# Row-wise cosine similarity: a split first load, separate half sums, and another engine that frees y

## The chip, the cores and the metric

The kernel runs on one core of a Trainium2 chip. The core has a TensorE (PE in the profile), a VectorE (DVE), a ScalarE (ACT), a GpSimd (POOL) and a SyncE (SP), which run their own instruction streams and meet through semaphores, and 16 DMA engines that move data between the HBM and the SBUF. The metric is the time of one execution on the device in microseconds (us), here the median of three runs.

## The reference

```python
def reference(x, y):                    # both 8192 x 8192 float32
    x_norm = np.linalg.norm(x, axis=1, keepdims=True)
    y_norm = np.linalg.norm(y, axis=1, keepdims=True)
    return np.sum(x * y, axis=1) / (x_norm.squeeze() * y_norm.squeeze() + 1e-8)
```

For every row three sums are needed: of x squared, of y squared, and of x times y. Each input element is read once; the inputs are 537 MB together, the output is 32 KB.

## The kernel before

**Tiling.** The 8192 rows are cut into 64 blocks of 128. The first 60 blocks are worked on in 30 groups of two blocks: each of the 128 partitions holds two neighbouring rows, 16,384 values or 65,536 bytes, so that one load brings 8.4 MB. The loads alternate, x of a group, then y of it, and go into three SBUF buffers `slot0` to `slot2` in turn (load m goes to slot m % 3). The last four blocks (b = 0 to 3) have one row to a partition; x lies in the first half of a slot and y in the second, and they are loaded in pieces (`PIECES`): whole halves at first, 13 pieces from 3968 down to 384 columns in the last block.

**Who does what.** ScalarE squares and sums x and y (`square`, L142, the ACTIVATE with its accumulator read). VectorE multiplies x with y and sums (`dot`, L145), and writes its products over x. The two rows of a partition have to give two separate sums, and a slot has to come free early: so VectorE first copies the last 4096 values of x into the PSUM tile `side` (L212). When y has come, it works off the middle 4096 values (second row, first half, into `part`), the first 8192 (first row), and then `side` with the last 4096 of y. The last of these starts from `part`, so that its sum is that of the whole second row. After the second of the three dots nothing reads x any more, and `used` tells SP that the slot is free. After the third dot, and when ScalarE has squared y, VectorE increments `used` for y's slot (L223).

**Loops and tokens.** The main part is four hardware loops over R = 10 rounds of three groups (nine rounds on SP), one on each of SP, TensorE, ScalarE and VectorE. `take` (L139) waits for a semaphore and takes the amount off again. SP takes one `used` for each load that it issues. TensorE, which has no arithmetic there, waits for each landing and hands a token to ScalarE (`for_act`) and one to VectorE (`for_dve`). ScalarE takes its token, squares the two halves of the slot, waits for each, and increments `x_squared` or `y_squared`; VectorE waits for `x_squared` ahead of the first dot, because this overwrites x, for its own `partial` around the last dot, and for `y_squared` at the end.

**After the loops.** Waits and increments are counted by hand (class `Queue`): `wait` is queued on an engine in program order, `done` gives an instruction's mark. SP issues the last blocks' loads when slots come free (`take_slot`: blocks 0 to 2 by `used` at 4, 5 and 6, block 3 by the marks of block 0). During block 0 the groups' results are made: the root of the square sums on ScalarE (L340), then on VectorE the product of the norms, plus EPS, the reciprocal (`reciprocal`, L263 to L270) and the multiplication with the dots (L344), two transposes on TensorE (L350), and two copies out of the PSUM on VectorE (L353). After block 2, ScalarE issues their store (L357). In the last block, after piece 4, the denominators of blocks 0 to 2 are made in the same way. The last piece's dot starts from the sum of the pieces before (`base`, L300), and short steps on ScalarE, VectorE and TensorE lead to the last store on SP.

**The opening.** `first_load_and_last_wait` moves the first load's DMA instruction into the opening block of the program, ahead of the barrier of all engines there, and the waits for the stores into the closing block.

The lines that a sentence can't say:

```python
    def take(engine, s, n=1):
        engine.wait_ge(s, n).then_inc(s, -n)
...
                dot(xt[:, K:CUT], yt[:, K:CUT], part, xt[:, K:CUT]).then_inc(partial, 1)
                dot(xt[:, 0:K], yt[:, 0:K], gsum[:, XY, r, c:c + 1], xt[:, 0:K]).then_inc(
                    used, 1)
```

## Time and profile before

| | |
|---|---|
| median of three runs | 1249.38 us (1249.23 to 1249.70) |
| the profiled execution | 1249.41 us, of which its span 1247.6 us |
| ScalarE busy | 916.9 us, 73% of the span |
| VectorE busy | 698.2 us, 56% |
| TensorE, GpSimd busy | 1.3 us, 0.8 us |
| share of 16 DMA engines' span taken by the loads' packets | 99.6% |
| HBM read | 536.87 MB, 430 GB/s over the span |
| a square of 8192 values, a dot of 8192, a dot of 4096, the copy of 4096 | 7.03, 8.69, 4.43, 4.43 us |

The page of a profile gives each engine's busy time, the span in 40 slices, the DMA queues, the chain of work that ended last, and the costliest groups of instructions with the idle time ahead of each and what ended it. A timeline lists instructions in order: start, duration (both in us), engine, line of the kernel, operation, operands, and in brackets the idle time before it with its releaser. SPq and ACTq are instructions of these engines' sequencers: a DMA's issue, a wait, a branch. A DMA's issue has a duration there, but the data move afterwards. A window's row gives, for a stretch of time, busy times of the engines, and at the end the DMA engines' share and the GB/s, where a packet counts whole at its start.

### The profile page before, as it was taken

What the parts mean: (1) busy time and instruction counts of PE and PEld (TensorE: products, weight loads), DVE (VectorE), ACT (ScalarE), POOL (GpSimd) and SP (SyncE); (2) the same over time, 40 slices, a digit from 0 to 9 for tenths busy, and PEclk for the clock granted to TensorE, in tenths of its full rate; (3) what the DMA queues carried; (4) which work ended last, traced back from release to release, by engine and by line L of the source; (5) the groups of instructions that cost most, each with busy time, mean ns of one, the idle gap of its engine ahead of it and who ended that gap; (6) DMA issues with size and microseconds to landing.
All of it is one profiled execution on the core that took longest, in us unless ns stands there. A gap on an engine that the chain in (4) does not pass through costs nothing. (4 is left out here: it accounts for less than half of the span.)

```text
span 1247.6 us, 1785 instructions
## 1 busy us (share of the span) xinstructions
PE 1.3 (0%) x4; PEld 0.3 (0%) x4; DVE 698.2 (56%) x252; ACT 916.9 (73%) x285; POOL 0.8 (0%) x8
## 2 busy tenths in 40 slices
PE   0000000000000000000000000000000000000000
PEld 0000000000000000000000000000000000000000
DVE  1654576545765447654467544675446755457566
ACT  3686776867768668677686776867868668677888
POOL 0000000000000000000000000000000000000000
DMA  9999999999999999999999999999999999999998
GB/s 435 431 414 435 437 437 437 437 435 435 433 412 437 437 437 437 437 437 435 435 424 420 437 437 437 437 437 437 433 433 412 437 437 437 437 437 437 418 425 335
DMA packets 11575, 536.93 MB, mean 430 GB/s; under 512 B 1299, under 2 KB 1845, under 8 KB 2613
## 3 DMA queue, kind: packets, MB, share of 16 engines
q1 hardware_dynamic: 11528, 536.88, 99.6%
q10 hardware_dynamic: 45, 0.03, 0.0%
q14 instruction: 2, 0.02, 0.0%
HBM read 536.87 MB, written 0.03 MB: 430 GB/s over the span
## 5 line engine op out<-in xcount | busy, mean ns | idle before, releaser
L142 ACT ACTIVATE junk<-slot 128x8192 uint8<-128x8192 f32 (+4 forms) x138 | 900.8, 6528 | 326.2 <-ACTq L139 320.5
L145 DVE CUSTOM_DVE_ANT_0 slot<-slot,slot 128x4096 f32<-128x4096 f32 (+1 forms) x60 | 391.1, 6556 | 452.4 <-DVEq L139 452.4
L212 DVE COPY side<-slot 128x4096 f32<-128x4096 f32 x30 | 132.8, 4428 | 71.7 <-DVEq L139 71.7
L145 DVE CUSTOM_DVE_ANT_0 side<-side,slot,part 128x4096 f32<-128x4096 f32 x30 | 134.6, 4488 | 0.0
L145 DVE CUSTOM_DVE_ANT_0 slot<-slot 128x8192 f32<-128x8192 f32 (+3 forms) x5 | 29.6, 5944 | 20.4 <-ACT junk L142 12.7
L142 ACT ACTIVATION_READ_ACCUMULATOR junk<-slot (+1 forms) x138 | 25.7, 186 | 0.0
L145 DVE CUSTOM_DVE_ANT_0 vjunk<-slot 128x384 uint8<-128x384 f32 (+4 forms) x8 | 6.8, 886 | 1.0 <-DMA slot<-in_y_dram 1.0
L145 DVE DVE_READ_ACCUMULATOR2_ANT gsum<- x60 | 6.7, 112 | 0.0
L145 DVE DVE_READ_ACCUMULATOR2_ANT part<- 128x1 f32 x30 | 2.5, 83 | 0.0
L192 ACT ACT_TABLE_LOAD x1 | 1.3, 1283 | 1.0 <-SPq L168 1.0
L350 PE MATMUL side<-ident,gden 128*30 128x128 f32 x2 | 0.6, 395 | 1196.9 <-DVE gden L344 1196.9
L194 ACT ACT_TABLE_LOAD x1 | 1.3, 1283 | 0.1
L145 DVE DVE_READ_ACCUMULATOR2_ANT parts<- 128x1 f32 x11 | 0.9, 82 | 0.0
L353 DVE COPY orow<-side 30x128 f32<-30x128 f32 x2 | 0.5, 279 | 0.6 <-PE side L350 0.6
L371 ACT COPY dots<-side 4x128 f32<-4x128 f32 x1 | 0.3, 254 | 0.7 <-PE side L369 0.7
L145 DVE CUSTOM_DVE_ANT_0 vjunk<-slot,base 128x384 uint8<-128x384 f32 x1 | 0.6, 619 | 0.1
L381 DVE TENSOR_TENSOR orl<-side,dots 4x128 f32<-4x128 f32 x1 | 0.3, 279 | 0.5 <-PE side L379 0.5
L270 DVE RECIPROCAL gden<-gden 128x60 f32<-128x60 f32 x1 | 0.5, 529 | 0.0
L350 PEld LDWEIGHTS side<-ident,gden 128*30 128x30 f32 x2 | 0.1, 107 | 1196.8 <-issue 1196.8
L369 PE MATMUL side<-ident,bsum 128*4 128x128 f32 x1 | 0.4, 373 | 46.9 <-DVE bsum L145 46.9
L379 PE MATMUL side<-ident,bden 128*4 128x128 f32 x1 | 0.4, 374 | 0.0
L340 ACT ACTIVATE gnorm<-gsum 128x120 f32<-128x120 f32 x1 | 0.3, 302 | 0.0
(25 smaller groups left out, 4.4 us busy)
## 6 DMA issues: line engine op xcount, KB each, us to landing
slot<-in_x_dram SPq DMA_DIRECT2D x3, 4096.0 KB, 29.9
slot<-in_y_dram SPq DMA_DIRECT2D x2, 4096.0 KB, 32.2
slot<-in_y_dram SPq DMA_DIRECT2D x1, 2368.0 KB, 35.8
slot<-in_x_dram SPq DMA_DIRECT2D x1, 1984.0 KB, 32.3
slot<-in_y_dram SPq DMA_DIRECT2D x1, 1728.0 KB, 39.4
slot<-in_y_dram SPq DMA_DIRECT2D x1, 1600.0 KB, 35.7
slot<-in_x_dram SPq DMA_DIRECT2D x1, 1088.0 KB, 37.9
slot<-in_y_dram SPq DMA_DIRECT2D x1, 640.0 KB, 40.2
```

What stands on the lines that cost most here:

```text
L142: return nc.scalar.activation(out=into, in_=src, func=ACTF.Square, accum_out=acc)
L145: return nc.vector.tensor_tensor_reduce(out=into, in0=a, in1=b, scale=1.0, scalar=init, op0=ALU.mult, op1=ALU.add, accum_out=acc)
L192: nc.scalar.memzero(dummy).then_inc(squared, 1)
L194: nc.scalar.sqrt(out=dummy, in_=dummy).then_inc(squared, 1)
L212: nc.vector.tensor_copy(out=side, in_=xt[:, CUT:])
L270: return dve.done(nc.vector.reciprocal(out=den, in_=den))
L340: m_norm = act.done(nc.scalar.activation(out=gnorm, in_=flat(gsum)[:, 0:2], func=ACTF.Sqrt))
L350: mk = pe.done(nc.tensor.transpose(out=t, in_=gden[:, j:2 * G:2], identity=ident))
L353: rows.append(dve.done(nc.vector.tensor_copy(out=orow[:, :, j], in_=t)))
L369: m_xy = pe.done(nc.tensor.transpose(out=psl[0], in_=bsum[:, XY, :], identity=ident))
L371: m_dots = act.done(nc.scalar.copy(out=dots, in_=psl[0]))
L379: mk = pe.done(nc.tensor.transpose(out=psl[1], in_=bden, identity=ident))
```

## The change

- The first load is cut into 16 partitions (`HEAD`) and 112, two DMAs with a semaphore each, and both issues are moved into the opening block. TensorE waits for the first semaphore once, ahead of its loop.
- The middle dot writes to a column of its own per group (`gpart`) in place of `part`; the last dot of a group starts from zero. GpSimd adds `gpart` to the second rows' sums once, at the end.
- In VectorE's loop the waits for `partial`, `x_squared` and `y_squared` and the increment of `used` for y go. The copy increments `x_done`, the last dot `y_done`.
- ScalarE's loop waits for its first half alone; the second increments `x_done` or `y_done`.
- TensorE takes two of `x_done` before it hands on the tokens for a y, two of `y_done` after that, and then increments `used` for y's slot.
- ScalarE waits for `used` to reach 6 before it goes on to the last blocks.
- The product of the norms and the addition of EPS go from VectorE to GpSimd (`denominator`), as does the multiplication of the groups' results; the reciprocals stay on VectorE, that of the groups in block 1, that of the last blocks after piece 6.
- The two copies of the groups' rows go from VectorE in block 0 to ScalarE after block 2, ahead of the store's issue.

```diff
-    load = next(i for i in body.instructions if i.opcode == "DMACopy")
+    loads = [i for i in body.instructions if i.opcode == "DMACopy"][:2]
...
-    opening.instructions = head[:at] + [load] + head[at:]
+    opening.instructions = head[:at] + loads + head[at:]
...
+    HEAD = 16
...
-        load(xg[0, 0], 0)
+        nc.sync.dma_start(out=slots[0][0:HEAD], in_=xg[0, 0, 0:HEAD]).then_inc(first, 16)
+        nc.sync.dma_start(out=slots[0][HEAD:], in_=xg[0, 0, HEAD:]).then_inc(landed[0], 16)
...
+        nc.tensor.wait_ge(first, 16)
         with nc.tensor.Fori(0, R):
             for m in range(2 * SLOTS):
                 take(nc.tensor, landed[m % SLOTS], 16)
+                if m % 2:
+                    take(nc.tensor, x_done, 2)
                 nc.tensor.sem_inc(for_act, 1)
                 nc.tensor.sem_inc(for_dve, 1)
+                if m % 2:
+                    take(nc.tensor, y_done, 2)
+                    nc.tensor.sem_inc(used, 1)
...
-                for j in range(2):
-                    square(s[:, j * K:(j + 1) * K], gsum[:, q, r, c + j:c + j + 1]).then_inc(
-                        squared, 1)
-                    take(nc.scalar, squared)
-                nc.scalar.sem_inc(y_squared if m % 2 else x_squared, 1)
+                square(s[:, 0:K], gsum[:, q, r, c:c + 1]).then_inc(squared, 1)
+                take(nc.scalar, squared)
+                square(s[:, K:], gsum[:, q, r, c + 1:c + 2]).then_inc(
+                    y_done if m % 2 else x_done, 1)
...
-                nc.vector.tensor_copy(out=side, in_=xt[:, CUT:])
+                nc.vector.tensor_copy(out=side, in_=xt[:, CUT:]).then_inc(x_done, 1)
                 take(nc.vector, for_dve)
-                take(nc.vector, x_squared)
-                dot(xt[:, K:CUT], yt[:, K:CUT], part, xt[:, K:CUT]).then_inc(partial, 1)
+                dot(xt[:, K:CUT], yt[:, K:CUT], gpart[:, r, a:a + 1], xt[:, K:CUT])
                 dot(xt[:, 0:K], yt[:, 0:K], gsum[:, XY, r, c:c + 1], xt[:, 0:K]).then_inc(
                     used, 1)
-                take(nc.vector, partial)
-                dot(side, yt[:, CUT:], gsum[:, XY, r, c + 1:c + 2], side, part).then_inc(
-                    partial, 1)
-                take(nc.vector, partial)
-                take(nc.vector, y_squared)
-                nc.vector.sem_inc(used, 1)
+                dot(side, yt[:, CUT:], gsum[:, XY, r, c + 1:c + 2], side).then_inc(y_done, 1)
...
+        act.wait((used, 2 * SLOTS))
...
-        def reciprocal(norm, den, squared, dotted):
-
-            dve.wait(squared, dotted)
-            m = dve.done(nc.vector.tensor_mul(out=den, in0=norm[:, 0], in1=norm[:, 1]))
-            dve.wait(m)
-            m = dve.done(nc.vector.tensor_scalar_add(out=den, in0=den, scalar1=EPS))
-            dve.wait(m)
+        def denominator(norm, den, *marks):
+
+            pool.wait(*marks)
+            m = pool.done(nc.gpsimd.tensor_mul(out=den, in0=norm[:, 0], in1=norm[:, 1]))
+            pool.wait(m)
+            return pool.done(nc.gpsimd.tensor_scalar_add(out=den, in0=den, scalar1=EPS))
+
+        def reciprocal(den, mark):
+            dve.wait(mark)
             return dve.done(nc.vector.reciprocal(out=den, in_=den))
...
-                    m_den = reciprocal(bnorm[:, :, 0:last], bden[:, 0:last], m_norm, m_sum)
+                    m_den = denominator(bnorm[:, :, 0:last], bden[:, 0:last], m_norm)
+                if b == last and n == 6:
+                    m_den = reciprocal(bden[:, 0:last], m_den)
...
-                m_g = reciprocal(gnorm, gden, m_norm, marks[-1])
-                dve.wait(m_g)
-                m_g = dve.done(nc.vector.tensor_mul(
+                m_g = denominator(gnorm, gden, m_norm)
+                odd = gsum[:, XY].rearrange("p r (a j) -> p r a j", j=2)[:, :, :, 1]
+                pool.wait(marks[-1])
+                m_odd = pool.done(nc.gpsimd.tensor_add(out=odd, in0=odd, in1=gpart))
+            if b == 1:
+                m_g = reciprocal(gden, m_g)
+                pool.wait(m_g, m_odd)
+                m_g = pool.done(nc.gpsimd.tensor_mul(
                     out=gden, in0=flat(gsum)[:, XY], in1=gden))
...
-                    dve.wait(mk)
-                    rows.append(dve.done(nc.vector.tensor_copy(out=orow[:, :, j], in_=t)))
+                    act_late.append((t, mk, orow[:, :, j]))
...
             if b == 2:
+                for t, mk, into in act_late:
+                    act.wait(mk)
+                    rows.append(act.done(nc.scalar.copy(out=into, in_=t)))
```

## The prediction

> **What bounds the kernel now.** I read the page first (engine shares, the forty slices, the queues), then the timeline of the first 75 us, then that of the last 100 us, then the chain that ended last. From the page:

> ```profile
> span 1247.6 us, 1785 instructions
> PE 1.3 (0%) x4; PEld 0.3 (0%) x4; DVE 698.2 (56%) x252; ACT 916.9 (73%) x285; POOL 0.8 (0%) x8
> ...
> q1 hardware_dynamic: 11528, 536.88, 99.6%
> ```

> The sixteen DMA engines are busy for 99.6% of the span; ScalarE has 27% to spare and VectorE 44%. So the inputs' transfer is the bound, and an edit in the loops counts only if it starves or slows that queue. The start of the timeline gives its pace:

> ```profile
> 0.00 0.41 SPq L150 DMA_DIRECT2D slot<-in_x_dram  x1
> ...
> 22.36 7.03 ACT L142 ACTIVATE junk<-slot 128x8192 uint8<-128x8192 f32 x1 [18.25 <-ACTq L139]
> ...
> 41.73 7.03 ACT L142 ACTIVATE junk<-slot 128x8192 uint8<-128x8192 f32 x1 [4.93 <-ACTq L139]
> ...
> 55.31 0.35 SPq L150 DMA_DIRECT2D slot<-in_y_dram  x1
> ...
> 59.99 0.34 SPq L150 DMA_DIRECT2D slot<-in_x_dram  x1
> 61.03 7.03 ACT L142 ACTIVATE junk<-slot 128x8192 uint8<-128x8192 f32 x1 [4.86 <-ACTq L139]
> 61.13 4.43 DVE L212 COPY side<-slot 128x4096 f32<-128x4096 f32 x1 [1.64 <-DVEq L139]
> ```

> Loads are worked on as they land, at 22.36, 41.73 and 61.03: one load of 128 rows x 65,536 B every 19.33 us, 434 GB/s. With eight rows to an engine that is 2.42 us for a row. A y load was issued into the freed x slot at 55.31, 5.7 us before the running load ended, and the next x load at 59.99: the queue always holds more than it is working on. From the last stage:

> ```profile
> 1227.41 0.19 ACT L142 ACTIVATION_READ_ACCUMULATOR junk<-slot 128x1 f32 x1
> 1227.70 3.51 ACT L142 ACTIVATE junk<-slot 128x3968 uint8<-128x3968 f32 x1
> ...
> 1231.53 2.87 ACT L142 ACTIVATE junk<-slot 128x3200 uint8<-128x3200 f32 x1 [0.22 <-DMA slot<-in_y_dram]
> ...
> 1237.89 1.27 ACT L142 ACTIVATE junk<-slot 128x1280 uint8<-128x1280 f32 x1 [0.26 <-DMA slot<-in_y_dram]
> ...
> 1242.49 0.51 ACT L142 ACTIVATE junk<-slot 128x384 uint8<-128x384 f32 x1
> ...
> 1243.33 0.17 DVE L300 TENSOR_REDUCE base<-parts 128x3 f32<-128x21 f32 x1
> ```

> ScalarE follows the landings with gaps of 0.2 to 0.3 us, and the reduction at 1243.33 needs its last pieces. Here a late ScalarE does cost.

> [...]

> **The change, part by part.** The sum is made against the profiled execution: 1249.41 us, of which 1247.6 are span and 1.8 lie around it. The median of the three runs is 1249.38, the same for this purpose.

> *First load.* One issue of 0.41 us becomes two, the second (0.33 us, by the following issues) also ahead of the opening's barrier. SP therefore issues y's first load some 0.3 us later than at 1.07; x's load ahead of it takes about 20 us, so nothing notices. ScalarE's table loads move by the same 0.3 us, and it waits 18.25 us afterwards. Gain: windows of half a microsecond count 1966 GB/s at 1.0 to 1.5 us, by the start of each packet; that is 15 of the 16 first rows. A shorter issue can bring the first rows forward by no more than its own 0.41 us; I take 0.2, between nothing and 0.4.
> Cost: the first 16 rows go to partitions 0 to 15. [...]
> The other 112 rows are seven for each engine[...]. I take 2.4 and keep 0 and 9.7 for the range. An engine's delay stays: each has the same 0.5 GB share / 16 to move afterwards at the same rate, never idle.
> Sum of this part: 7.7 + 2.4 - 0.2 = +9.9.

> *Loops.* VectorE loses two waits for itself and two for ScalarE in each of 30 groups, ScalarE one wait per load and a semaphore instruction; the sums go to two columns. The dots have the same sizes (4.43, 8.69, 4.49 us). All lies under the transfer: VectorE already idles 1.64 us ahead of its copy and ScalarE 4.9 ahead of each load. Gain nothing. The added waits are TensorE's. For x: ScalarE has squared it at 36.80 and VectorE copied it at 26.88, y lands near 41.7, 4.9 us of cover. For y: VectorE's last dot ends near 59.5, the next x lands at 61.0, 1.5 us of cover. Queued behind that wait are the tokens for both engines on the next x; if the cover went, they would start late by the excess, and the next slots come free later. Even then there is a whole load (19.3 us) issued at 55.31. Nothing.

> *Hand-over.* ScalarE now waits for the sixth `used`, after VectorE's last dot (1182.26), in place of starting at 1179.34: some 3.3 us later. Its four squares and the root then run to about 1211.7, and the third block's x lands at 1213.07; 1.4 us remain. VectorE's dot of block 0 ends near 1198.6 in place of 1195.3, so SP issues the last block's loads from 1198.7. Seven issues of 0.47 bring it to 1202, and it was blocked from 1198.17 to 1214.19 [...] anyway. Nothing.

> *Group results.* VectorE's three operations leave it and three (with the joining addition, four) arrive on GpSimd, which is free. Bounds for each: 0.1 us (its memsets) and 1 us. They start near 1197 and, after the reciprocal, near 1214; ScalarE reads the transposes only after 1227.6. Thirteen microseconds of cover.
> The two row copies go to ScalarE just ahead of the last block: 0.25 us each (the L371 copy of the same kind is 0.25), and the store's issue, 0.64 us at 1222.87, must now wait for them. ScalarE's accumulator read ends at 1227.60; two copies to 1228.1, issue to 1228.75, so the 3968 square starts near 1228.8 and not 1227.70: +1.1. The gaps behind it (0.3 at 3200, 0.25 at 1280, 0.15 over the following) take back about 0.7. The second-last 384 square ends near 1243.5 and not 1243.09, the reduction starts near 1243.6 and not 1243.33: +0.3. Bounds: 0 and 0.6.

> *Last denominators.* Two VectorE operations of 0.17 go to GpSimd; the reciprocal comes after the dot of 1280 columns, ahead of a 0.53 us idle stretch. GpSimd at 0.5 each gives 1239.7, in time. At 1 us each VectorE would be some 0.3 late at the end. I take nothing.

> Sum: 1249.4 + 9.9 + 0.3 = 1259.6 us.

> **The rivals.**
> 1. [...] the 16 rows cost 2.42 us as before. For it: the trace shows 27.1 GB/s per engine[...]. Then only the start and ScalarE's tail remain: 1249.4 - 0.2 + 0.3 = 1249.5, with 1248.8 to 1250.1. This is the not-slower side; it decides if the first 16 rows take below some 5 us.
> 2. *The 112 rows are dealt out in turn*, row 16 + 16t + e to engine e. [...] For it: nothing in the profile excludes an order. [...]
> 3. *TensorE's ordered waits starve the queue.* A token more than 1.5 us late would hold both engines in each of 30 groups. If it ate the whole 5.7 us as well, each further 0.1 us costs 3 us. Against it: a relay of a few semaphore instructions; the timelines show gaps of 0.02 to 0.09 us for such steps. One microsecond beyond the cover would be 1279.

> **How the numbers follow.** [...] engines set the pace 0.34, dealt in turn 0.05, TensorE 0.02; the remaining 0.01 is a start that loses most of the 3.0 us by which the first load lands beyond its 19.33. A difference under 0.2% (2.5 us) is about what a measurement of this kernel can't tell from none. Faster 0.02 (the last case and an unknown of rival 1), same 0.33, slower 0.65. The range takes in rival 1 and the contention's own range: 1248.8 to 1267.

> **What would show it.** Right: ScalarE's first square near 32 us or later in place of 22.36, later loads again at 19.3 us apart, the same lateness at the end. Wrong: a first square at 22 to 23 us. The tail: a 3968 square 1.1 us behind its landing, the reduction waiting for ScalarE. TensorE's step: VectorE's copy starting later than 0.2 us behind ScalarE's square of the same x.

## The result, and the profile after

The changed kernel takes 1270.62 us (median of five runs, 1270.42 to 1270.87) against 1249.39 for the kernel before: 1.0169 times its time, 95% interval 1.0155 to 1.0183, 21.2 us more. The profiled execution has a span of 1268.5 us in place of 1247.6.

From the page of the changed kernel: its span, the engines' busy time, the GB/s of the forty slices (31.7 us each), and the loads' queue. The last line is the GB/s of the kernel before, by its own slices (31.2 us).

```profile
span 1268.5 us, 1634 instructions
PE 1.3 (0%) x4; PEld 0.3 (0%) x4; DVE 694.8 (55%) x245; ACT 916.8 (72%) x287; POOL 4.7 (0%) x14
...
GB/s 223 364 432 432 430 430 432 432 430 432 448 432 434 432 430 430 434 430 432 446 434 434 432 430 430 434 430 430 446 434 436 432 430 430 434 430 430 434 427 331
...
q1 hardware_dynamic: 11544, 536.88, 99.6%
...
GB/s 435 431 414 435 437 437 437 437 435 435 433 412 437 437 437 437 437 437 435 435 424 420 437 437 437 437 437 437 433 433 412 437 437 437 437 437 437 418 425 335
```

The share of the queue's packets, 99.6%, is the same as before, and would suggest that nothing has changed: a packet that is held up counts as busy (by the trace's single packets the first sixteen took 7.52 to 9.25 us each, in the kernel before 2.48 to 3.42). The GB/s tell it. The first slice moved 223 and the second 364, every later one about as much as before. The loss lies in the first 45 us. The timeline of the start of the changed kernel:

```profile
0.00 0.41 SPq L172 DMA_DIRECT2D slot<-in_x_dram  x1
...
0.46 0.40 SPq L173 DMA_DIRECT2D slot<-in_x_dram  x1
...
44.14 7.03 ACT L144 ACTIVATE junk<-slot 128x8192 uint8<-128x8192 f32 x1 [39.57 <-ACTq L141]
...
63.67 7.03 ACT L144 ACTIVATE junk<-slot 128x8192 uint8<-128x8192 f32 x1 [5.09 <-ACTq L141]
...
82.83 7.03 ACT L144 ACTIVATE junk<-slot 128x8192 uint8<-128x8192 f32 x1 [4.72 <-ACTq L141]
82.93 4.43 DVE L222 COPY side<-slot 128x4096 f32<-128x4096 f32 x1 [1.56 <-DVEq L141]
```

The first square starts at 44.14, not 22.36: 21.8 us late. The following two come 19.5 and 19.2 us apart, as before, and VectorE idles 1.56 us ahead of its copy (1.64 before). Windows of the same kernel (start and end, length, busy times of the engines; at the end the clock, the DMA engines' share and the GB/s), and last one of the kernel before:

```profile
2.00:10.00 8.00, 0.00 (x0) 0.00 (x0) 0.00 (x0) 2.44 (x4) 0.34 (x3) 1.00 0.44 74
11.00:21.00 10.00, 0.00 (x0) 0.00 (x0) 0.00 (x0) 0.00 (x0) 0.00 (x0) 1.00 0.81 210
21.00:31.00 10.00, 0.00 (x0) 0.00 (x0) 0.00 (x0) 0.00 (x0) 0.00 (x0) 1.00 0.89 223
...
11.00:21.00 10.00, 0.00 (x0) 0.00 (x0) 0.00 (x0) 0.00 (x0) 0.00 (x0) 1.00 0.98 426
```

A packet counts whole where it starts, so a short window's rate is rough. But where the kernel before moved 426 GB/s from 11 to 21 us, this one moves 210, and 223 in the next ten: not only the first 16 rows are slow, the 112 behind them run at half pace.

The tail of the changed kernel, at the place that the prediction spoke of:

```profile
1248.31 0.19 ACT L144 ACTIVATION_READ_ACCUMULATOR junk<-slot 128x1 f32 x1
1248.40 0.41 ACT L372 COPY orow<-side 30x128 f32<-30x128 f32 x2
1248.84 0.64 ACTq L374 DMA_DIRECT2D out_dram<-orow  x1
...
1249.59 3.51 ACT L144 ACTIVATE junk<-slot 128x3968 uint8<-128x3968 f32 x1 [0.78 <-ACT orow L372]
```

The two copies and the store's issue stand between the squares, and the 3968 square starts 1.09 us after the end of the accumulator read.

### The profile page after: what moved, and what is told of

The parts are those of the page before. It is cut to its first block, busy times and chain, and to the rows that moved or that the text cites. A ratio compares the mean times of both kernels' runs of the same rounds, so it can differ in the third digit from the quotient of the medians.

```text
span 1268.5 us, 1634 instructions
## 1 busy us (share of the span) xinstructions
PE 1.3 (0%) x4; PEld 0.3 (0%) x4; DVE 694.8 (55%) x245; ACT 916.8 (72%) x287; POOL 4.7 (0%) x14
## 3 DMA queue, kind: packets, MB, share of 16 engines
q1 hardware_dynamic: 11544, 536.88, 99.6%
## 5 line engine op out<-in xcount | busy, mean ns | idle before, releaser
L147 DVE CUSTOM_DVE_ANT_0 side<-side,slot 128x4096 f32<-128x4096 f32 x30 | 132.9, 4429 | 0.0
L147 DVE CUSTOM_DVE_ANT_0 slot<-slot 128x8192 f32<-128x8192 f32 (+3 forms) x5 | 29.6, 5944 | 22.8 <-ACT junk L144 22.8
## 6 DMA issues: line engine op xcount, KB each, us to landing
slot<-in_y_dram SPq DMA_DIRECT2D x2, 4096.0 KB, 31.9
```

The source lines that it names most:

```text
L147: return nc.vector.tensor_tensor_reduce(out=into, in0=a, in1=b, scale=1.0, scalar=init, op0=ALU.mult, op1=ALU.add, accum_out=acc)
```

## The experiments

Two theories at the start: the split costs it, by the partitions that each part reaches; or the new waits, the hand-over and the tail hold part of it. Within the first, the slow side could be SBUF or the HBM.

In the kernels with a "written out" loop, VectorE's hardware loop is ten rounds one after the other, with the same work; in those with "fixed sums", its loop is kept, its sums go to a fixed tile, and one or two small copies per round move them on.

**The split undone, and the split alone.** The changed kernel with `load(xg[0, 0], 0)` again, and the kernel before with the split; VectorE's loop is written out in both. Of the second edit the two loads are shown; as in the changed kernel, both issues move into the opening and TensorE waits for `first`.

```diff
-        load(xg[0, 0], 0)
+        nc.sync.dma_start(out=slots[0][0:16], in_=xg[0, 0, 0:16]).then_inc(first, 16)
+        nc.sync.dma_start(out=slots[0][16:], in_=xg[0, 0, 16:]).then_inc(landed[0], 16)
```

> The changed kernel with the first load whole again (one DMA, alone in the opening; no `first`); VectorE's loop is written out round by round, which changes none of its work. Theory (the split alone costs the 21 us, by its partitions): 1249.4, within 0.7, first square near 22.4 us. Rival (the new waits of TensorE, the hand-over or the tail hold part of it): 1255 or more, with a first square still near 22 us. ScalarE's later start on the last block should leave its reduction 0.3 us later than its landings of before.

> The kernel before with the split of 16 and 112 partitions alone (VectorE's loop written out). Theory: the whole loss, 1270.6 within 1, first square near 44 us. Rival (the other edits take part in it): 1265 or less.

Measured: with the first load whole 1251.48 us (1.0015, 1.0008 to 1.0022), first square at 22.66; with the split alone 1272.36 us (1.0184, 1.0167 to 1.0201), first square at 44.12. The split holds the loss of some 20 us. But both are some 2 us above what was expected, and whether the other edits had part in those 2 us was open.

**Another split.** The same 1.05 MB first, but as 2048 columns on all partitions; and the load in two halves of 64 partitions, which isn't shown (both again with VectorE's loop written out):

```diff
-        load(xg[0, 0], 0)
+        nc.sync.dma_start(out=slots[0][:, 0:2048], in_=xg[0, 0, :, 0:2048]).then_inc(first, 16)
+        nc.sync.dma_start(out=slots[0][:, 2048:], in_=xg[0, 0, :, 2048:]).then_inc(landed[0], 16)
```

> The kernel before with its first load split as well, but by columns: 2048 of 16384 columns on all 128 partitions first (the same 1.05 MB), then the rest; both issues in the opening, VectorE's loop written out. Theory (partitions): [...] no loss: 1249.4 within 0.6, first square near 22.4. Rival (two DMAs in a row in the opening, or a small first DMA, cost by themselves): 1255 to 1270.

> The kernel before with its first load split into partitions 0 to 63 and 64 to 127 (VectorE's loop written out). Theory [...]: each half takes twice its time, 38.7 us in place of 19.4, so +19.4: 1268.8, first square near 41.7. Rival (the HBM side: sixteen engines reading sixteen neighbouring rows are what is slow): here an engine has four rows of its own, so little or nothing, 1249 to 1254.

Measured: by columns 1252.80 us (1.0025, 1.0015 to 1.0034), first square at 22.18; by halves 1273.68 us (1.0194, 1.0177 to 1.0211), first square at 43.67. The halves came 5 us above the 1268.8 expected, 3 of which the next experiment finds in the written-out loop. Against that loop alone (1252.55), two DMAs of all partitions cost nothing, two DMAs of 64 partitions 21 us. The first issue takes 0.41 us with 2048 columns as well.

**What the 2 us were.** The kernel before with nothing but the loop written out, and, with the loops kept and fixed sums, the kernel before, the changed kernel with a whole first load, and the same with the split by columns:

```diff
-        with nc.vector.Fori(0, R) as r:
+        for r in range(R):
```

```diff
-                dot(side, yt[:, CUT:], gsum[:, XY, r, c + 1:c + 2], side, part).then_inc(
+                dot(side, yt[:, CUT:], gacc[:, c + 1:c + 2], side, part).then_inc(
...
+            nc.vector.tensor_copy(out=gsum[:, XY, r, :], in_=gacc).then_inc(partial, 1)
+            take(nc.vector, partial)
```

> The kernel before with VectorE's loop written out and nothing else. Theory (the 2 us of the whole-first-load run come from the longer instruction stream, whose fetches take DMA time, and not from the changed waits): 1251.0 to 1251.9, with four or five instruction packets in place of two. Rival (they come from the other edits of the change): 1249.4 to 1249.8.

> The kernel before with its loops kept, VectorE's sums of a round in a fixed tile that one copy per round moves on. The copy lies in VectorE's idle time. Theory (fetches): two instruction packets again, 1249.4 within 0.5. Rival (anything that delays the loops' hand-overs shows at once): 1251 or more.

> The changed kernel with a whole first load, loops kept, VectorE's sums of a round in a fixed tile moved on by two copies per round. Theory (all edits but the split are hidden): the same as the kernel before with fixed sums, within 0.6; of this 0 to 0.6 for ScalarE's later last block. Rival (they cost or gain beyond it): 1250.5 or more, or below 1248.8.

> As the changed kernel with fixed sums, with the first load split by columns (2048 on all 128 partitions, then the rest). Theory: the first packets start no earlier (an issue takes 0.41 us for 16 rows as for 128), so 0 to 0.3 below the whole first load. Rival (a small first load starts the engines sooner): 0.4 or more below it. A count below 1248.8 would beat both kernels.

| kernel | median, us | ratio to before, 95% interval |
|---|---|---|
| before, loop written out | 1252.55 | 1.0025 (1.0015 to 1.0035) |
| before, fixed sums | 1249.46 | 1.0000 (0.9992 to 1.0009) |
| changed, whole first load, fixed sums | 1249.43 | 1.0000 (0.9991 to 1.0009) |
| changed, split by columns, fixed sums | 1249.45 | 1.0000 (0.9991 to 1.0009) |

The 2 us belong to the written-out loop and not to the change. In the kernel before it costs more than expected, 3.1 us (1252.55 against 1249.46); in the changed kernel with a whole load 2.1 (1251.48 against 1249.43). Beside the written-out kernel before, the split by partitions costs 19.8 us (1272.36), not 21.2: the two losses don't simply add, and why is open. From the page of the written-out kernel before, the queues:

```profile
q1 hardware_dynamic: 11528, 536.88, 99.5%
q14 instruction: 5, 0.04, 0.0%
```

Five instruction packets in place of two; that the fetches alone make the 3 us was argued, not shown. With the loops kept, all edits but the split together change nothing that can be measured: 1249.43 against 1249.46. The split by columns brings nothing either: no version here beats the kernel before.

**Single loads.** Three kernels put ten extra loads of whole rows into `slot0` ahead of the first load of the kernel before (loop written out). Each kernel ran once, but loads that stand in more than one of them agree: all 128 partitions 21.8 to 22.0 us, 16 to 127 32.8 and 33.3, every fourth 7.6 and 8.1. Each waits for the one before, so that the issues of SP's timeline stand one landing apart; the kernel's own load then writes over them.

```diff
...
+        nc.sync.dma_start(out=slots[0][0:16], in_=xg[0, 0, 0:128:8]).then_inc(probed, 16)
+        nc.sync.wait_ge(probed, 48)
...
         load(xg[0, 0], 0)
```

> The kernel before with ten extra loads into slot0 ahead of its own, each alone (SP waits for its landing), of full rows of 65,536 B; the results are loaded over. VectorE's loop is written out. Time from issue to landing by the theory ([...] about 2.5 us fixed): all 128: 22. Partitions 0 to 15 from rows 0 to 15: 12 [...]. Partitions 0 to 15 from rows 0, 8, 16 and so on: 12. Partitions 0, 8, 16 and so on from rows 0 to 15: 7 [...]. The same from rows 0, 8, 16: 7. Partitions 0 to 31: 12. 0 to 63: 22. 64 to 127: 22. Every second partition: 22 or less. Every fourth partition: 7 to 12. Rival (the HBM side: neighbouring rows read at once): the time follows the rows read, so the third probe is like the fifth (4.5 to 7), and the fourth like the second (12).

> As the first probe kernel, with other partitions, always from the rows of the same number. Theory with each engine taking neighbouring rows: all 128: 22. Partitions 16 to 127: 25 to 32 (it took 31 behind the first 16 in the changed kernel); 0 to 111: the same. 0 to 95 and 32 to 127 (six rows an engine): 17 to 27. 0 to 79 and 48 to 127 (five rows): 15 to 25. 0 to 119 [...]: 22 to 40. 0 to 3 [...]: 12. 0 to 7 [...]: 12. Rival (112 rows are slow only because the 16 before them have put the engines out of step): 16 to 127 alone takes 17 + 2.5 = 19.5. Rival [...]: four rows in 5.

SP's timeline of the first of these kernels (the extra loads in the order in which the expectation names them; the last line is the kernel's own):

```profile
0.00 0.42 SPq L171 DMA_DIRECT2D slot<-in_x_dram  x1
22.01 0.35 SPq L173 DMA_DIRECT2D slot<-in_x_dram  x1
33.75 0.32 SPq L175 DMA_DIRECT2D slot<-in_x_dram  x1
45.25 0.62 SPq L177 DMA_DIRECT2D slot<-in_x_dram  x1
52.88 0.51 SPq L179 DMA_DIRECT2D slot<-in_x_dram  x1
60.70 0.32 SPq L181 DMA_DIRECT2D slot<-in_x_dram  x1
73.00 0.49 SPq L183 DMA_DIRECT2D slot<-in_x_dram  x1
95.82 0.48 SPq L185 DMA_DIRECT2D slot<-in_x_dram  x1
118.61 0.49 SPq L187 DMA_DIRECT2D slot<-in_x_dram  x1
131.31 0.48 SPq L189 DMA_DIRECT2D slot<-in_x_dram  x1
138.94 0.35 SPq L150 DMA_DIRECT2D slot<-in_x_dram  x1
```

In the second of these kernels, from SP's issues again: partitions 16 to 127 alone 32.8 us, 0 to 111 32.2, 0 to 95 31.8, 32 to 127 31.9, 0 to 79 27.4, 48 to 127 27.1, 0 to 119 42.3, 0 to 3 11.4, 0 to 7 11.2. All the loads of 80 to 120 rows lie above their expected ranges, by up to 5 us. So 112 rows take longer than 128, by themselves and without 16 rows ahead of them, and with 96 and 80 rows every sixteen cost over 5 us (31.8 / 6, 27.4 / 5). Are all rows of such a load slow, or do some run on at 2.42 us? The last of these kernels asks for that, with sixteen rows at a time:

> As the earlier probes[...]. One row per engine, so that no order of dealing matters. Partitions 0, 5, 10 and so on to 75[...]. 0, 7 and so on to 105[...]. 0, 6 and so on to 90 and 16, 23 and so on to 121[...]. Theory A [...]: rows of two lengths, about 4.5 to 5.1 us and 2.4 to 3.2 us[...]; issue to landing 7.6 for all, by the slowest row. Theory B [...]: all rows near 4.5 to 5.1. For the loads of many rows: partitions 0 to 47 (three rows an engine) 17 to 18 us by B [...]; 16 to 127 again 32 to 33; 16 to 111 near 32; every fourth partition 7.6.

Windows of that kernel, one for each extra load, up to its landing (columns as above): all 128 partitions; every fifth from 0; every seventh from 0; every sixth from 0; every seventh from 16; 0 to 15; 0 to 47; every fourth; 16 to 127; 16 to 111.

```profile
0.00:21.90 21.90, 0.00 (x0) 0.00 (x0) 0.00 (x0) 2.97 (x4) 0.80 (x8) 1.00 0.92 383
21.90:29.30 7.40, 0.00 (x0) 0.00 (x0) 0.00 (x0) 0.00 (x0) 0.00 (x0) 1.00 0.64 142
29.30:36.30 7.00, 0.00 (x0) 0.00 (x0) 0.00 (x0) 0.00 (x0) 0.00 (x0) 1.00 0.63 150
36.30:43.50 7.20, 0.00 (x0) 0.00 (x0) 0.00 (x0) 0.00 (x0) 0.00 (x0) 1.00 0.63 146
43.50:50.70 7.20, 0.00 (x0) 0.00 (x0) 0.00 (x0) 0.00 (x0) 0.00 (x0) 1.00 0.63 146
50.70:62.50 11.80, 0.00 (x0) 0.00 (x0) 0.00 (x0) 0.00 (x0) 0.00 (x0) 1.00 0.72 89
62.50:88.90 26.40, 0.00 (x0) 0.00 (x0) 0.00 (x0) 0.00 (x0) 0.00 (x0) 1.00 0.90 119
88.90:97.00 8.10, 0.00 (x0) 0.00 (x0) 0.00 (x0) 0.00 (x0) 0.00 (x0) 1.00 0.71 259
97.00:130.40 33.40, 0.00 (x0) 0.00 (x0) 0.00 (x0) 0.00 (x0) 0.00 (x0) 1.00 0.91 220
130.40:162.00 31.60, 0.00 (x0) 0.00 (x0) 0.00 (x0) 0.00 (x0) 0.00 (x0) 1.00 0.92 199
```

Share times length times 16 engines is the time of all packets together, and divided by the rows it is that of one. Every seventh partition from 0: 0.63 x 7.0 x 16 = 71 us for 16 rows, 4.4 us each; every fifth comes to 4.7 (0.64 x 7.4), the other two to 4.5 (0.63 x 7.2). Had, for example, twelve of the sixteen run free at about 2.9 (every fourth partition: 0.71 x 8.1 x 16 / 32) and four at 4.7, the sum would be 54 us and the share 0.48. So here most rows, if not all, are slow, as theory B has it; a mean doesn't tell if a few were quicker.

The same sum gives 8.5 us a row for partitions 0 to 15, 7.9 for 0 to 47, 4.3 for 16 to 127. The load of 0 to 47 missed its forecast: 26.4 us against 17 to 18. Why is open.

In the changed kernel the 112 rows can be followed step by step. Windows of it, each with the starts of sixteen rows, one step (178 GB/s in 5.90 us are 1.05 MB), so that share times length is the mean time of a row:

```profile
8.90:14.80 5.90, 0.00 (x0) 0.00 (x0) 0.00 (x0) 0.00 (x0) 0.00 (x0) 1.00 0.91 178
14.80:19.50 4.70, 0.00 (x0) 0.00 (x0) 0.00 (x0) 0.00 (x0) 0.00 (x0) 1.00 1.01 223
19.50:22.80 3.30, 0.00 (x0) 0.00 (x0) 0.00 (x0) 0.00 (x0) 0.00 (x0) 1.00 1.01 318
22.80:26.60 3.80, 0.00 (x0) 0.00 (x0) 0.00 (x0) 0.00 (x0) 0.00 (x0) 1.00 1.00 276
26.60:30.90 4.30, 0.00 (x0) 0.00 (x0) 0.00 (x0) 0.00 (x0) 0.00 (x0) 1.00 1.05 244
30.90:35.50 4.60, 0.00 (x0) 0.00 (x0) 0.00 (x0) 0.00 (x0) 0.00 (x0) 1.00 1.02 228
35.50:40.00 4.50, 0.00 (x0) 0.00 (x0) 0.00 (x0) 0.00 (x0) 0.00 (x0) 1.00 1.02 233
```

The third and fourth steps are the quick ones: 3.3 and 3.8 us a row, the others 4.5 to 5.4. By the trace's single packets, the rows of the first, second and last three took 4.26 to 5.71 us; fourteen rows of the third step took 2.9 to 3.3 us and two took 4.8; in the fourth, fourteen took 3.5 to 3.7 and two 4.4 and 4.6. So within one load there are steps in which all sixteen rows are slow, as theory B has it, and steps with rows of two lengths, as theory A has it, though the fourteen quick ones too stayed above 2.42 us. What decides between the two is open.

## Why the prediction was wrong

The prediction's likeliest case (0.58, own range 1256.7 to 1266.9) was that the two parts of the load are slowed by the partitions that each reaches in the SBUF. It is the one that happened, and the direction was right; its size was not: 1259.6 forecast, 1270.62 measured. Its terms for the slow rows rested on nothing that the trace of the kernel before shows. By its steps:

*The first 16 rows: +7.7 forecast.* Alone they land in 11.7 us. A first row on all partitions would by estimate land in 22.0 - 7 x 2.42 = 5.1, so they cost 6.6. The term was nearly right. Over the window from 22.00 to 33.70 of the first of the single-load kernels these rows moved at 90 GB/s, all 128 partitions (0.00 to 22.00) at 381.

*The other 112 rows: +2.4 forecast, 0 to 9.7 allowed.* This is the term that failed. Alone they take 32.8 us; in the whole load's pace they would take 22.0 - 2.42 = 19.6: +13.2, above the upper bound. The 2.4 is one row's time more, as if nearly all rows ran on at 2.42 us. In the changed kernel all sixteen rows took 4.26 us or more in five of the seven steps, and in the other two the fourteen quick ones still took 2.9 to 3.7. And of the two bounds I took a value near the lower one with no row of the profile behind it.

*The sum.* 6.6 + 13.2 = 19.8 of the 21.8 by which the first square is late. The remaining 2 us weren't taken apart; the two parts and the next load follow each other there, with the engines out of step: by the trace's packets the last sixteen rows of the load start over 2.3 us (35.60 to 37.86), in the kernel before over 0.6 (18.55 to 19.16).

*The start: -0.2 forecast.* Nothing. The issue takes 0.41 us for 16 rows as for 128, so there was nothing to gain by it; the split by columns is no faster either (1249.45 against 1249.43).

*The loops and TensorE's waits: nothing forecast.* Right: 1249.43 against 1249.46 with everything but the split, and VectorE's idle time ahead of its copy is nearly unchanged (1.56 us, 1.64 before).

*The hand-over: 3.3 us, hidden.* Right. In the changed kernel with a whole load and fixed sums ScalarE starts the last blocks at 1182.76, SP issues the last block's loads from 1198.84 (1198.7 forecast), and ScalarE still waits 1.14 us for the third block's x (1.4 forecast). From the timeline of that kernel:

```profile
1182.76 7.03 ACT L143 ACTIVATE junk<-slot 128x8192 uint8<-128x8192 f32 x1 [3.98 <-PEq L197]
...
1198.84 0.33 SPq L299 DMA_DIRECT2D slot<-in_x_dram  x1
...
1212.79 7.03 ACT L143 ACTIVATE junk<-slot 128x8192 uint8<-128x8192 f32 x1 [1.14 <-DMA slot<-in_x_dram]
...
1243.29 0.52 ACT L143 ACTIVATE junk<-slot 128x384 uint8<-128x384 f32 x1 [0.34 <-DMA slot<-in_y_dram]
...
1243.49 0.17 DVE L309 TENSOR_REDUCE base<-parts 128x3 f32<-128x21 f32 x1
```

*The tail: +0.3.* The step is there: the 3968 square begins 1.09 us after the accumulator read, 0.10 before, so 1.0 late against 1.1 forecast. What is left of it at the end is within the noise of the runs: by the last lines above ScalarE waits for its data again ahead of the last piece, so it has caught up, and the reduction starts at 1243.49 against 1243.33 before. GpSimd's operations took up to 1.40 us, over my bound of 1 us; their cover was large enough.

*The rivals.* That engines set the pace fell at once: a row of the first sixteen took 7.52 us or more, not 2.42. Rows dealt out in turn would go to sixteen neighbouring partitions at a time, by estimate from the load of 0 to 15 alone some 8.5 us a row; 4.3 were measured. TensorE's waits starving the queue: no sign of it.

## What to carry to other kernels

Let a load reach all 128 partitions at once: here the split by partitions cost 21.2 us. If a first piece has to be small, cut its columns, which cost nothing here (1249.45 us against 1249.43), though it brought nothing either. The part of 112 partitions wasn't seven eighths of the cost of 128 but one and a half times it (32.8 against 22.0 us); what slows it wasn't shown. Stores weren't tried. A bound on rows that slow one another must say what happens to the rest: where the profile can't tell, take it that all are slowed, and let the range reach there.

## What the runs showed of the hardware

- Single loads of neighbouring partitions: 120 took 42.3 us, 96 took 31.8, 64 took 22.8, 48 took 26.4: five us or more for every sixteen rows, against 2.75 with all 128 (22.0 us). Every second partition (12.7 us for 64 rows) and every fourth (7.6 for 32) took 3.2 and 3.8 for every sixteen.
- Sixteen rows into every seventh partition from 0 took 4.4 us each on average. In the changed kernel's 112 rows all sixteen rows took 4.26 to 5.71 us in five of the seven steps; in the third and fourth, fourteen took 2.9 to 3.7 and two 4.4 to 4.8.
- As the first in the program, an issue on SP took 0.41 us for 16 or for 128 rows (0.58 for 64).
- In the changed kernel GpSimd took 1.40 us for a product of 60 columns and 1.36 us for an addition of three, but 0.25 to 0.37 us for other operations as small as these.
- Writing out VectorE's loop cost 3.1 us (1252.55 against 1249.46), with five instruction packets in place of two, on DMA engines whose packets fill 99.5% of the span.
